# Two-layer hybrid decoder trunk: second-half operands of the way up made in chunks on VectorE, a third pair of weight columns begun early, and products added in PSUM

## The chip, the cores and the metric

The kernel runs on one core of a Trainium2 chip. The engines are TensorE (PE in the profile, with PEld for its weight loads), VectorE (DVE), ScalarE (ACT), GpSimd (POOL) and SyncE (SP), which issues nearly all transfers. The metric is the device time of one execution in microseconds (us), lower is better. Before the change it is 2558.94 us, the median of 3 runs from 2552.66 to 2560.61.

## What is computed

The reference is a decoder trunk of two layers over 1024 positions and 1024 features in float32. Each layer adds a mixer, then a SwiGLU feed-forward block, then a gated embedding. The change touches the feed-forward block alone, in both layers:

```python
def swiglu(h, w_gate, w_up, w_down):
    return (jax.nn.silu(h @ w_gate) * (h @ w_up)) @ w_down
...
h = h + swiglu(rmsnorm(h, g_ffn[layer]), w_gate[layer], w_up[layer], w_down[layer])
```

`w_gate` and `w_up` are 1024 x 2816, `w_down` is 2816 x 1024. The two products with `w_gate` and `w_up` are called the way up here, the one with `w_down` the way down.

## The kernel before

**Numbers.** Every float32 operand of a matmul is split in two parts that TensorE takes in a faster format: hi, a rounded copy made by ScalarE (line 146), and lo, the rest, a subtraction (line 147, on VectorE unless an engine is named). A product of two split operands is three matmuls (`mm3`, lines 205 to 207): hi by hi, hi by lo, lo by hi.

**The way up as a 2 x 2 block product with seven products in place of eight.** The positions form two halves of 512, the 1024 features two halves of 512, and the 2816 columns two halves of 1408, that is 11 columns `i` of 128 in each half. For one `i` and one of gate and up (a *column* below, `d` in the code) four output tiles of 128 x 512 are made, called 11, 12, 21 and 22, by the Winograd scheme: sums and differences of the four weight quarters (units 1 to 7 in `w_seven`) times sums and differences of the four operand quarters (`XC[1]` to `XC[7]`). One product is 4 feature tiles x 3 matmuls = 12 matmuls of 128 x 128 by 128 x 512, into one PSUM bank (`prod`, line 520). A layer has 22 columns (11 gate, 11 up) and 154 products. A gate column and its up column make a pair.

**Operands.** `XC[1]` and `XC[2]` depend only on the first half of the positions; they are ready before the way up begins. `XC[3]` to `XC[7]` also need the second half, whose norm factor `R[1]` is ready only some products into the way up: the two matmul groups `rs` and `Rb` of that norm run between the first products. `second_half` (line 470) then scales the eight second-half tiles (`normed`, line 437), makes the differences and splits 20 operands. Some of that is on VectorE (lines 483 and 485 and most lower halves), some on GpSimd (lines 488 and 495, four lower halves of `XC[4]` and two of `XC[3]`).

**Order.** Because of this wait, `ffn_up` (line 501) begins two pairs, four columns (called a0 to a3 here: gate and up of i = 0, gate and up of i = 1), with the two products that need only the first half: `p1` (its result is copied from PSUM by ScalarE, line 574) and `p2` (added to that copy by VectorE into output tile 11). `second_half` is written between them. Then each of the four gets its other weight units (`w_seven`) and its products 6, 3, 7, 5, 4 (`p6` and `rest`). From i = 2 on every column does 1, 6, 2, 3, 7, 5, 4 in one go. After every product an add on VectorE takes its bank: `u` lines 526 and 586, `sg` line 535 for gate, `act` line 540 for up. A gate tile then gets its SiLU on ScalarE (line 536), an up tile is multiplied with the gate tile on GpSimd (line 542), and `operands` stores the tiles and four differences of them (line 554, GpSimd, tiles `at`) to device memory for the way down.

**Weights.** `w_seven` loads four quarters of 256 KB, which wait for one of six buffers `raw`; GpSimd makes s1, s3, s2 and s4 (lines 184, 186, 188, 193); ScalarE and VectorE split seven units into eight pairs of buffers `whi` and `wlo`. A `raw` buffer is free again when its unit is split, a `whi` buffer when its product is done. For a0 to a3 `w_first` has made units 1 and 2 already.

**Buffers around it.** PSUM has six banks for products. Six temporaries `t` of 128 x 512 hold `p1`, `u`, `t2` and others. `slot` names fixed places; the gate tiles `sg` and the differences `at` share places 56 to 63, the up tiles stand in 64 to 68.

Instructions keep their order within an engine; which order that is, a planner fixes beforehand from the order of the program and its own estimate of durations, so a later instruction may be put ahead of one that it expects to be held up. At run time an engine waits at an instruction until what it needs is there.

Of the kernel before, what the change touches and what calls it, by code (L numbers as in the profile page):

```python
# [11 lines left out]
F32 = mybir.dt.float32  # L12
# [4 lines left out]
ALU = mybir.AluOpType  # L17
# [4 lines left out]
P = 128  # L22
# [24 lines left out]
class Build:  # L47
# [125 lines left out]
    def w_seven(self, w, c0, c1, name, u=None):  # L173
# [15 lines left out]
        u[6] = self.w_halves(s2, name)  # L189
        if not have:  # L190
            u[2] = self.w_halves(a12, name)
        s4 = a12
        tt(out=s4, in0=a12, in1=s2, op=ALU.subtract)
        u[3] = self.w_halves(s4, name)
        u[7] = self.w_halves(s3, name)
        u[5] = self.w_halves(s1, name)
        u[4] = self.w_halves(a22, name)
        return u

    def mm3(self, ps, a, b, first, last):

        mm = self.nc.tensor.matmul
        mm(ps, a[0], b[0], start=first, stop=False)  # L205
        mm(ps, a[0], b[1], start=False, stop=False)  # L206
        mm(ps, a[1], b[0], start=False, stop=last)  # L207

    def part_mm(self, ps, unit, op, first, last):
        n = len(unit)  # L210
        for k in range(n):
            self.mm3(ps, unit[k], op[k], first and k == 0, last and k == n - 1)
        self.tick()

    def ws_mm(self, ps, unit, kt, op, order=None):
# [125 lines left out]
def trunk(ctx, tc, x, p, positions, g_mix, g_ffn, g_ple, ev_w_in, ev_w_conv, ev_g_v, ev_w_s,  # L341
# [85 lines left out]
    def mixer_out(w, mix, res_d, h_d, gcol, order=None, begun={}, then=None):  # L427
# [40 lines left out]
        free = iter(list(range(32, 54)) + list(range(16, 32)) + [54, 55])  # L468

        def second_half():  # L470
            def made(key, x, eng):
                i = next(free)
                t = B.slots2(i, next(free), "xc")
                B.split(t[0], t[1], x, eng)
                XC[key].append(t)

            ks = range(4)
            t2s = []
# [12 lines left out]
            for k in ks:  # L491
                made(7, h[1][k], nc.vector)
            for k in ks:
                c = h[0][k + 4]
                nc.gpsimd.tensor_tensor(out=c, in0=c, in1=t2s[k], op=ALU.subtract)
                made(5, h[0][k], nc.vector)
            for k in ks:
                made(4, h[0][k + 4], nc.gpsimd)
        return XC, second_half

    def ffn_up(l, XC, second_half, act_d, behind):
# [2 lines left out]
        sg, act = {}, {}  # L504
        c2 = lambda i: slice(i * P, (i + 1) * P)

        def start(i, up, first=False):
            d = {"i": i, "up": up, "w": (w_gate, w_up)[up][l]}
            if first:
                d["u"] = B.w_first(d["w"], c2(i), "gu"[up])  # L510
            else:
                seven(d)
            return d
# [5 lines left out]
        def prod(d, k):  # L519
            ps = B.ps(f"p{k}")  # L520
            B.part_mm(ps, d["u"][k], XC[k], True, True)
            return ps

        def plus(a, b, name):
            t = B.tmp(name)
            nc.vector.tensor_tensor(out=t, in0=a, in1=b, op=ALU.add)
            return t

        def out(d, key, a, b):

            i, n = d["i"] + (half if key[0] == "2" else 0), int(key[1]) - 1
            j = int(key[0]) * 2 - 2 + n
            if not d["up"]:
                s = sg[i, n] = B.slot(56 + (d["i"] % 2) * 4 + j, F32, "sg")
                nc.vector.tensor_tensor(out=s, in0=a, in1=b, op=ALU.add)
                nc.scalar.activation(s, s, AF.Silu)
                return
            t = B.slot(68 if j == 0 and d["i"] % 2 else 64 + j, F32, "act")
            act[d["i"], key] = t
            nc.vector.tensor_tensor(out=t, in0=a, in1=b, op=ALU.add)  # L540
            last = d["i"] == half - 1
            (nc.vector if last else nc.gpsimd).tensor_tensor(  # L542
                out=t, in0=t, in1=sg[i, n], op=ALU.mult
            )
            operands(d["i"], key)

        def operands(i, key):


            keep = lambda k, t: nc.sync.dma_start(act_d[k][i], t)  # L550
            spare = lambda j: B.slot(56 + (i + 1) % 2 * 4 + j, F32, "at")

            def minus(t, a, b):
                nc.gpsimd.tensor_tensor(out=t, in0=a, in1=b, op=ALU.subtract)
                return t

            if key == "22":
                keep(2, act[i, "22"])
            elif key == "12":
                keep(1, act[i, "12"])  # L560
                act[i, "t1"] = minus(spare(1), act[i, "11"], act[i, "12"])
                keep(5, act[i, "t1"])
            elif key == "21":
                b = act[i, "21"]
                keep(3, b)
                t2 = minus(spare(2), b, act[i, "t1"])
                keep(6, t2)
                keep(7, minus(act[i, "11"], b, act[i, "11"]))
                keep(4, minus(spare(3), act[i, "22"], t2))

        def p1(d):
            a = prod(d, 1)
            d["p1"] = B.tmp("p1")
            nc.scalar.copy(d["p1"], a)  # L574
# [19 lines left out]
        ahead = []  # L594
        for i in range(2):
            ds = [start(i, up, True) for up in range(2)]
            for d in ds:
                p1(d)
            if i == 0:
                second_half()  # L600
            for d in ds:
                p2(d)
            ahead += ds
        for d in ahead:
            seven(d)
            p6(d)
            rest(d)
        for i in range(2, half):
            for up in range(2):
                d = start(i, up)  # L610
                p1(d)
                p6(d)
                p2(d)
                rest(d)

    half = NFF // 2
# [1290 lines left out]
```

## Time and profile before

| | |
|---|---|
| time, median of 3 runs | 2558.94 us (2552.66 to 2560.61) |
| the profiled execution's time | 2558.38 us |
| its span | 2556.7 us |
| way up of layer 0, first product to first matmul of the way down | 353.9 to 800.0 us |
| way up of layer 1 | 1738.2 to 2183.8 us |
| 256 KB loads of `w_gate` and of `w_up` | 96 each, median 3.1 and 2.9 us from issue to landing |

The page gives for each engine its busy time, share of the span and number of instructions. The waits of an engine are lines "who <- for whom: us in total, times, longest". A row of the timeline is start, duration, engine, line, operation, output and inputs, count, and in brackets the idle time before it with what ended it. A matmul's duration is longer than its distance to the next, since matmuls overlap. A row of the windows is a stretch, its length, and the busy time and count of PE, PEld, DVE, ACT and POOL, then the granted clock, the share of the DMA engines and GB/s.

### The profile page before, as it was taken

How to read it: one execution, taken by the hardware profiler on the slowest of the kernel's cores; microseconds unless marked ns; L12 is line 12 of the kernel's file. 1: busy time of each engine (PE TensorE's matmuls, PEld its weight loads, DVE VectorE, ACT ScalarE, POOL GpSimd, SP SyncE). 2: the span in 40 equal slices, each digit the busy share in tenths (PEclk: the TensorE clock that was granted, in tenths of full speed). 3: DMA queues.
4: the chain of work that ended last, by engine and by line, in shares of the span. 5: the costliest groups of instructions: out<-in, count | busy, mean ns of one | idle time of the engine just before them, and what ended most of it. 6: DMA issues, size and time to landing. Idle time of an engine off the chain costs nothing.

```text
span 2556.7 us, 34220 instructions
## 1 busy us (share of the span) xinstructions
PE 2451.1 (96%) x11510; PEld 2017.8 (79%) x11510; DVE 1565.3 (61%) x2935; ACT 977.5 (38%) x1869; POOL 1007.8 (39%) x918
## 2 busy tenths in 40 slices
PE   8999998999999988999999999997999999988999
PEld 6878876788888776788888788886888888876777
DVE  6863487555556667676775466468565455676732
ACT  5322342333224434444454455543233233444421
POOL 3451146565552554212221122126655554255300
PEclk9999999999999998999999999998999999998999
DMA  4221532333327657553455733162323324766731
GB/s 145 91 74 49 158 120 87 109 111 98 111 93 230 220 188 232 177 176 92 110 149 154 195 97 105 46 184 69 127 91 113 110 92 135 233 222 204 262 107 39
DMA packets 352736, 345.53 MB, mean 135 GB/s; under 512 B 23691, under 2 KB 245232, under 8 KB 352560
## 3 DMA queue, kind: packets, MB, share of 16 engines
q1 hardware_dynamic: 352064, 343.00, 43.2%
q8 instruction: 91, 1.49, 0.2%
q0 software_dynamic: 464, 0.33, 0.1%
q14 instruction: 85, 0.70, 0.1%
q10 hardware_dynamic: 32, 0.01, 0.0%
HBM read 251.51 MB, written 91.75 MB: 134 GB/s over the span
## 4 chain that ended last, share of the span: by engine, by line
PE 67%; DVE 7%; DMA 4%; issue 2%; POOL 2%; ACT 1%; SPq 0%; DVEq 0%; POOLq 0%; ACTq 0%
PE p L205 10%; PE p L206 10%; PE p L207 9%; PE pd L205 4%; PE pd L206 3%; PE pd L207 3%; DMA rd<-in_w_down 3%; PE O L1795 2%; PE ppg L207 2%; PE ppg L205 2%; PE ppg L206 2%; PE PT L1837 1%; PE po L205 1%; PE po L206 1%; PE po L207 1%
## 5 line engine op out<-in xcount | busy, mean ns | idle before, releaser
L205 PE MATMUL pd<-acth,hd 128*128 128x512 f32 x616 | 248.5, 403 | 41.2 <-DVE res L690 29.3
L147 DVE TENSOR_TENSOR lu<-ru,hu 128x512 fp32r<-128x512 f32 x138 | 128.2, 930 | 210.8 <-ACT hu L146 210.5
L206 PE MATMUL pd<-actl,hd 128*128 128x512 f32 x616 | 246.2, 400 | 0.0
L207 PE MATMUL pd<-acth,ld 128*128 128x512 f32 x616 | 245.2, 398 | 0.0
L205 PE MATMUL p<-xch,hg 128*128 128x512 f32 x440 | 177.3, 403 | 21.1 <-ACT p L574 15.1
L275 POOL TENSOR_TENSOR S<-S,sq 128x512 f32<-128x512 f32 x62 | 89.1, 1436 | 274.3 <-ACT sq L273 273.2
L146 ACT CAST hu<-ru 128x512 fp32r<-128x512 f32 x138 | 82.9, 619 | 274.7 <-POOL ru L188 173.2
L206 PE MATMUL p<-xcl,hg 128*128 128x512 f32 x440 | 175.7, 399 | 2.7 <-DVE xcl L147 2.7
L205 PEld LDWEIGHTS pd<-acth,hd 128*128 128x128 f32 x616 | 119.7, 194 | 71.4 <-DVE res L690 32.5
L207 PE MATMUL p<-xch,lg 128*128 128x512 f32 x440 | 174.8, 399 | 0.2 <-DVE lg L147 0.2
L207 PE MATMUL p<-xch,lu 128*128 128x512 f32 x440 | 172.9, 393 | 0.0
L205 PE MATMUL p<-xch,hu 128*128 128x512 f32 x440 | 172.9, 393 | 0.0
L206 PE MATMUL p<-xcl,hu 128*128 128x512 f32 x440 | 172.6, 392 | 0.0
L147 DVE TENSOR_TENSOR ld<-rd,hd 128x512 fp32r<-128x512 f32 x110 | 99.5, 905 | 82.1 <-ACT hd L146 81.7
L147 DVE TENSOR_TENSOR actl<-ra,acth 128x512 fp32r<-128x512 f32 x154 | 142.3, 928 | 11.9 <-ACT acth L146 11.7
L147 DVE TENSOR_TENSOR lg<-rg,hg 128x512 fp32r<-128x512 f32 x132 | 110.8, 840 | 61.9 <-ACT hg L146 61.5
L146 ACT CAST hg<-rg 128x512 fp32r<-128x512 f32 x132 | 80.8, 619 | 177.1 <-POOL rg L188 56.6
L207 PEld LDWEIGHTS pd<-acth,ld 128*128 128x128 f32 x616 | 119.6, 194 | 25.8
L206 PEld LDWEIGHTS pd<-actl,hd 128*128 128x128 f32 x616 | 119.9, 195 | 24.6
L542 POOL TENSOR_TENSOR act<-act,sg 128x512 f32<-128x512 f32 x80 | 118.9, 1498 | 18.3 <-DVE act L540 9.7
L146 ACT CAST hd<-rd 128x512 fp32r<-128x512 f32 x110 | 68.4, 622 | 149.5 <-POOL rd L651 51.1
L205 PEld LDWEIGHTS p<-xch,hg 128*128 128x128 f32 x440 | 84.7, 193 | 42.3 <-ACT p L574 16.0
(552 smaller groups left out, 6787.6 us busy)
## 6 DMA issues: line engine op xcount, KB each, us to landing
rd<-in_w_down SPq DMA_DIRECT2D x198, 256.0 KB, 3.4
ra<-act SPq DMA_DIRECT2D x154, 256.0 KB, 3.1
rg<-in_w_gate SPq DMA_DIRECT2D x96, 256.0 KB, 3.1
ru<-in_w_up SPq DMA_DIRECT2D x96, 256.0 KB, 2.9
act<-act SPq DMA_DIRECT2D x88, 256.0 KB, 2.0
act<-at SPq DMA_DIRECT2D x66, 256.0 KB, 2.1
rpg<-in_w_ple_gate SPq DMA_DIRECT2D x48, 256.0 KB, 3.0
rwo<-in_ev_w_out SPq DMA_DIRECT2D x32, 256.0 KB, 2.8
```

The lines of the kernel that those rows point to most:

```text
L146: self.nc.scalar.copy(hi, src)
L147: (eng or self.nc.vector).tensor_tensor(out=lo, in0=src, in1=hi.bitcast(F32), op=ALU.subtract)
L205: mm(ps, a[0], b[0], start=first, stop=False)
L206: mm(ps, a[0], b[1], start=False, stop=False)
L207: mm(ps, a[1], b[0], start=False, stop=last)
L275: eng.tensor_tensor(out=st[n], in0=st[n], in1=sq, op=ALU.add)
L542: (nc.vector if last else nc.gpsimd).tensor_tensor(out=t, in0=t, in1=sg[i, n], op=ALU.mult)
L1795: nc.tensor.matmul(O[h][:, b * DV : (b + 1) * DV], t[:, j * P : (j + 1) * P], V[h // 2][:, kb, (h % 2) * DV : (h % 2 + 1) * DV], start=kb ...
L1837: nc.tensor.transpose(pt[:, j * P : (j + 1) * P], e[:, j * P : (j + 1) * P], ident)
```

## The change

It has these parts:

- `second_half` becomes a generator of nine chunks. All its subtractions and splits use VectorE (and ScalarE for the hi parts); none uses GpSimd. Chunks 1 to 4 make `XC[6]`, two more `XC[7]`, one each `XC[5]`, `XC[4]`, `XC[3]`. The caller runs a chunk after nearly every first product.
- A third pair (i = 2, `third`) is begun early as well. Order of the first products: p1 of a0 to a3, p2 of a0 to a3, then p1, p1, p2, p2 of the third pair. Its p1 copies and its tile 11 are kept in `raw` buffers and stored to device memory (`early`), and loaded again when the pair is finished, after a3.
- p2 is accumulated onto p1's PSUM bank, after ScalarE has copied p1 out of it; tile 11 is read straight from that bank (`out11`). Product 4 is accumulated onto product 7's bank and product 3 onto product 5's, each after VectorE has read that bank. Two adds per column go.
- Products come in the order 6, 7, 5, 4, 3; `w_seven` makes unit 3 last; the four differences in `operands` are all made after tile 12, now the last one.

```diff
@@ second_half
+            minus = lambda o, a, b: nc.vector.tensor_tensor(out=o, in0=a, in1=b, op=ALU.subtract)
             for k in ks:
                 normed(1, k)
                 normed(1, k + 4)
-                a, b, d = h[0][k], h[1][k], h[1][k + 4]
-                nc.vector.tensor_tensor(out=a, in0=b, in1=a, op=ALU.subtract)
+                a, b, c, d = h[0][k], h[1][k], h[0][k + 4], h[1][k + 4]
+                minus(a, b, a)
                 t2 = B.tmp("t2")
-                nc.vector.tensor_tensor(out=t2, in0=d, in1=a, op=ALU.subtract)
-                t2s.append(t2)
-                made(6, t2, nc.vector)
-                nc.gpsimd.tensor_tensor(out=b, in0=d, in1=b, op=ALU.subtract)
+                minus(t2, d, a)
+                made(6, t2)
+                minus(c, c, t2)
+                yield
             for k in ks:
-                made(3, h[1][k + 4], (nc.vector, nc.gpsimd)[k % 2])
-            for k in ks:
-                made(7, h[1][k], nc.vector)
-            for k in ks:
-                c = h[0][k + 4]
-                nc.gpsimd.tensor_tensor(out=c, in0=c, in1=t2s[k], op=ALU.subtract)
-                made(5, h[0][k], nc.vector)
-            for k in ks:
-                made(4, h[0][k + 4], nc.gpsimd)
+                minus(h[1][k], h[1][k + 4], h[1][k])
+                made(7, h[1][k])
+                if k % 2:
+                    yield
+            for key, x in ((5, h[0][0:4]), (4, h[0][4:8]), (3, h[1][4:8])):
+                for t in x:
+                    made(key, t)
+                yield
...
@@ ffn_up
+        def out11(d, t):
+            if not d["up"]:
+                nc.scalar.activation(t, d["X"], AF.Silu)
+                sg[d["i"], "11"] = t
+            else:
+                nc.vector.tensor_tensor(out=t, in0=d["X"], in1=sg[d["i"], "11"], op=ALU.mult)
+                act[d["i"], "11"] = t
...
+        def p1(d, t):
+            d["X"], d["p1"] = prod(d, 1), t
+            nc.scalar.copy(t, d["X"])
         def p2(d):
-            out(d, "11", prod(d, 2), d["p1"])
+            prod(d, 2, d["X"])
         def p6(d):
-            d["u2"] = plus(prod(d, 6), d["p1"], "u2")
+            u2 = d["p1"]
+            nc.vector.tensor_tensor(out=u2, in0=prod(d, 6), in1=u2, op=ALU.add)
         def rest(d):
-            u2 = d["u2"]
-            u4 = plus(prod(d, 3), u2, "u4")
-            p7 = prod(d, 7)
-            nc.vector.tensor_tensor(out=u2, in0=p7, in1=u2, op=ALU.add)
+            u2 = d["p1"]
+            pa = prod(d, 7)
+            u3 = B.tmp("u3")
+            nc.vector.tensor_tensor(out=u3, in0=pa, in1=u2, op=ALU.add)
             if d["up"] and d["i"] == half - 1:
                 behind()
-            p5 = prod(d, 5)
-            out(d, "22", p5, u2)
-            out(d, "12", p5, u4)
-            out(d, "21", prod(d, 4), u2)
+            pb = prod(d, 5)
+            out(d, "22", pb, u3)
+            prod(d, 4, pa)
+            out(d, "21", pa, u2)
+            prod(d, 3, pb)
+            out(d, "12", pb, u2)
...
+        for d in ahead:
+            first(d)
+        for j, d in enumerate(ahead):
+            p1(d, B.tmp("p1"))
+            if j:
+                next(more)
+        for j, d in enumerate(ahead):
+            p2(d)
+            if j < 2:
+                first(third[j])
+            next(more)
+        seven(ahead[0])
+        for d, t in zip(third, early):
+            p1(d, raw("p1"))
+            nc.sync.dma_start(t, d["p1"])
+            next(more, None)
+        for d in third:
+            p2(d)
+            next(more, None)
+            out11(d, raw("o11"))
+        nc.sync.dma_start(early[2], act[2, "11"])
+        for _ in more:
+            pass
+        for d in ahead:
+            out11(d, spot(d, "11"))
+        for j, d in enumerate(ahead):
+            if j:
+                seven(d)
+            p6(d)
+            rest(d)
+        for d, t in zip(third, early):
+            seven(d)
+            d["p1"] = load(t, "p1")
+            p6(d)
+            if d["up"]:
+                t = act[2, "11"] = spot(d, "11")
+                nc.sync.dma_start(t, early[2])
+            rest(d)
+        for i in range(3, half):
             for up in range(2):
                 d = start(i, up)
-                p1(d)
+                seven(d)
+                p1(d, B.tmp("p1"))
                 p6(d)
                 p2(d)
+                out11(d, spot(d, "11"))
                 rest(d)
```

`first(d)` is `w_first` of the column, `seven(d)` is `w_seven`, `spot` names the slot of an output tile. In `prod(d, k, ps)` a given bank is accumulated onto.

More of the change, by code (lines that the diff above doesn't have):

```diff
@@ L505, in ffn_up, with start, first @@
         c2 = lambda i: slice(i * P, (i + 1) * P)
[L507 to L513, printed above, removed]
+        def start(i, up):
+            return {"i": i, "up": up, "w": (w_gate, w_up)[up][l]}
+        def first(d):
+            d["u"] = B.w_first(d["w"], c2(d["i"]), "gu"[d["up"]])
         def seven(d):
@@ L604, in ffn_up @@
-        for d in ahead:
-            seven(d)
+            pb = prod(d, 5)
[4 more added lines that the diff above has]
+            out(d, "12", pb, u2)
+        more = second_half()
+        ahead = [start(i, up) for i in range(2) for up in range(2)]
+        third = [start(2, up) for up in range(2)]
+        raw = lambda name: B.wp.tile([P, HT], F32, tag="raw", name=B.name(name), bufs=RAW)
+        early = [dp.tile([P, HT], F32, name=B.name("early")) for _ in range(3)]
```

85 lines of the change are left out of this document (34 added, 51 removed).

## The prediction

> **What bounds the kernel now.** I read the page first, then TensorE's waits, then the timeline of the way up.
>
> ```profile
> PE 2451.1 (96%) x11510; PEld 2017.8 (79%) x11510; DVE 1565.3 (61%) x2935; ACT 977.5 (38%) x1869; POOL 1007.8 (39%) x918
> ```
>
> TensorE is the bound. Nothing in the change removes a matmul, so the most it can win is TensorE's idle and slow time inside the two ways up (one per layer). TensorE's waits name it:
>
> ```profile
> PE p L205 <- ACT p L574: 15.1, 2, 7.6
> ...
> PE p L205 <- DVE sg L535: 6.0, 2, 3.0
> ...
> PE p L206 <- DVE xcl L147: 2.7, 2, 1.7
> ...
> PE p L205 <- DVE u L526: 0.9, 1, 0.9
> ```
>
> All but the last come twice, once per layer. The timeline gives their places (start, duration, then in brackets the idle time before it and who ended it):
>
> ```profile
> 353.88 0.39 PE L205 MATMUL p<-xbh,hg 128*128 128x512 f32 x1
> ...
> 357.61 1.02 PE L282 MATMUL rs<-ones_f,S 128*128 128x1 f32 x8 [0.85 <-DVE S L275]
> ...
> 365.39 0.39 PE L205 MATMUL p<-xbh,hu 128*128 128x512 f32 x1
> ...
> 378.76 0.39 PE L207 MATMUL p<-xbh,lu 128*128 128x512 f32 x1
> 386.72 0.80 PE L205 MATMUL p<-xch,hg 128*128 128x512 f32 x1 [7.57 <-ACT p L574]
> 387.31 0.63 PE L206 MATMUL p<-xcl,hg 128*128 128x512 f32 x1
> 387.74 0.63 PE L207 MATMUL p<-xch,lg 128*128 128x512 f32 x1
> ...
> 409.40 0.39 PE L205 MATMUL p<-xch,hu 128*128 128x512 f32 x1
> ...
> 1738.21 0.39 PE L205 MATMUL p<-xbh,hg 128*128 128x512 f32 x1
> ...
> 1794.44 0.39 PE L205 MATMUL p<-xch,hu 128*128 128x512 f32 x1
> ```
>
> The stage of layer 0 begins at 353.88, that of layer 1 at 1738.21. The fourth product starts at 365.39; product 8 starts its last matmul at 378.76, 59 matmuls on: 13.37 / 59 = 0.2266 us each, 2.72 us per product of 12. At 409.40 (and 1794.44) the second weight column, a1, starts product 6. By then 13 products are done: two first products of each of four columns, and five more of a0.
>
> Their price undisturbed: 13 x 2.72 = 35.4, plus what the norm of the second half inserts. That is 365.39 - 353.88 = 11.51 for three products (8.16): 3.35. Together 38.7. Measured are 55.5 in layer 0 and 56.2 in layer 1, so **16.8 and 17.5 us are lost** in idle time and slow matmuls (0.63 for 0.39). That is the prey.
>
> Why it idles: each column of a pair holds PSUM banks, six in all, and the fourth copy of product 1 (L574) and the adds L535/L540 come late.
>
> ```profile
> 384.52 1.66 ACT L146 CAST xch<-h 128x512 fp32r<-128x512 f32 x3 [1.17 <-POOL h L495]
> 386.09 0.57 ACT L574 COPY p<-p 128x512 f32<-128x512 f32 x1
> ...
> 364.59:398.20 33.61, 22.11 (x89) 17.16 (x87) 33.61 (x31) 15.61 (x26) 23.71 (x14) 0.90 0.03 9
> ...
> 364.59 1.41 DVE L437 SCALAR_TENSOR_TENSOR h<-h,vec,R 128x512 f32<-128x512 f32 x2 [0.66 <-ACT R L317]
> ...
> 390.61 1.75 DVE L147 TENSOR_TENSOR xcl<-t,xch 128x512 fp32r<-128x512 f32 x1
> 392.28 5.99 DVE L147 TENSOR_TENSOR xcl<-h,xch 128x512 fp32r<-128x512 f32 x8
> 398.20 0.68 DVE L535 TENSOR_TENSOR sg<-p,p 128x512 f32<-128x512 f32 x1
> ...
> 393.75 1.56 POOL L147 TENSOR_TENSOR xcl<-h,xch 128x512 fp32r<-128x512 f32 x1 [1.94 <-ACT xch L146]
> ```
>
> The copy stands behind casts that wait for POOL. In the windows row (PE, PEld, DVE, ACT, POOL: busy and count) VectorE is full for 33.61 us with 31 operations, 1.08 each, while POOL runs 14. Beside a POOL operation one takes 1.75; in the run of eight, with POOL's single L147 beside one of them, it is (5.99 - 1.7) / 7 = 0.61. So second-half operands cost VectorE about 0.6 alone and 1.7 beside POOL.
>
> **The change part by part.**
>
> *Operands on VectorE alone.* 44 operations (30 of the 31, whose last is already an add, and POOL's 14): 8 norms at 0.66 and 36 at 0.60 are 26.9 us with POOL quiet, against 33.6 now. The operands of product 6 are the first four chunks, 4 x (2 x 0.66 + 4 x 0.60) = 14.9 us.
>
> *Third pair begun early.* Four more products, 10.9 us, stand ahead of product 6 of a0. R comes about when it does now: 364.6. TensorE reaches product 6 at 353.9 + 3.35 + 12 x 2.72 = 389.9; its operands are there at 364.6 + 14.9 + 2.4 (four lower halves of the third pair's first weights) = 381.9. Product 7's follow at 386.7. The rest of the queue is 12 halves for products 5, 4, 3 (7.2) and five of a0's weights (3.0): 396.9, wanted at 389.9 + 4 x 2.72 = 400.8. So it fits by 4 us while POOL is quiet. POOL is not: `w_seven` of a0 and of a1 gives it eight subtractions here, each costing VectorE up to 1.75 - 0.61 = 1.1: 0 to 8.8.
>
> The Trainium skill, "SBUF — State Buffer", section "Who interferes with whom", says that a VectorE instruction with two SBUF inputs and a GpSimd one that reads SBUF block each other for the whole instruction; it would make this up to 8 x 1.29 = 10.3, and the rows show 1.1 a pair, a little less.
>
> *The supply of a1's weights.* In the trace they follow directly on a0's lower halves:
>
> ```profile
> 400.59 0.86 DVE L147 TENSOR_TENSOR lg<-rg,hg 128x512 fp32r<-128x512 f32 x1
> ...
> 406.35 1.29 POOL L188 TENSOR_TENSOR ru<-su,ru 128x512 f32<-128x512 f32 x1
> ```
>
> a0's halves (from 400.59) free the raw buffers, a1 is loaded, POOL ends its s2 at 407.64, TensorE starts at 409.40. After the change 17 products are done by then, undisturbed at 389.9 + 13.6 = 403.5, and a0's halves come before the operands of 4 and 3, near 391 to 399. So a1's product 6 lies between 403.5 and 409.4: a new wait of 0 to 5.9 per layer. I take 3.0, the middle.
>
> *A smaller gain.* S L275 takes long because POOL works on a0's weights:
>
> ```profile
> 355.69 1.77 DVE L275 TENSOR_TENSOR S<-S,sq 128x512 f32<-128x512 f32 x1
> ...
> 355.30 1.61 POOL L188 TENSOR_TENSOR rg<-sg,rg 128x512 f32<-128x512 f32 x1
> ```
>
> Now the third pair's first loads take those buffers, POOL comes later, and the 0.85 of idle time (357.61) should go: 0 to 0.85 per layer, taken whole.
>
> *Products added in PSUM.* p2 is added onto p1's bank, p4 onto p7's, p3 onto p5's. Two VectorE adds per column go; on VectorE, idle in the steady part, they are worth nothing. But TensorE gets three new waits per column: p2 for the copy of p1, p4 for the add that reads p7, p3 for the add that reads p5, each with one product of 2.7 us between. In the trace these readers are often later:
>
> ```profile
> 496.09 0.39 PE L207 MATMUL p<-xch,lg 128*128 128x512 f32 x1
> ...
> 506.36 0.69 DVE L147 TENSOR_TENSOR lu<-ru,hu 128x512 fp32r<-128x512 f32 x1 [10.82 <-ACT hu L146]
> 506.97 0.68 DVE L526 TENSOR_TENSOR u<-p,p 128x512 f32<-128x512 f32 x1
> ...
> 512.63 0.39 PE L207 MATMUL p<-xbh,lu 128*128 128x512 f32 x1
> ...
> 519.76 0.58 ACT L574 COPY p<-p 128x512 f32<-128x512 f32 x1
> ...
> 650.70 0.39 PE L207 MATMUL p<-xch,lg 128*128 128x512 f32 x1
> ...
> 656.52 0.68 DVE L526 TENSOR_TENSOR u<-p,p 128x512 f32<-128x512 f32 x1
> ...
> 667.24 0.39 PE L207 MATMUL p<-xbh,lu 128*128 128x512 f32 x1
> ...
> 669.37 0.58 ACT L574 COPY p<-p 128x512 f32<-128x512 f32 x1
> ```
>
> Product 6 of a gate column ends at 496.5, its add starts at 506.97, 10.5 late, behind a lower half of the next column that waits for POOL. Later in the stage it is 656.52 - 651.1 = 5.4. The copy of an up column's p1 is 519.76 - 513.0 = 6.8 late, later 669.37 - 667.6 = 1.7. Today six banks absorb this. Behind a waiting p2 or p4 stands all the rest of TensorE's queue, in order, and with it the next column's casts that wait for weight buffers. With the change p4's wait allows the first add some 6.2 us (three products less about two operations), the copy 2.2 (2.7 less its 0.58). So the steady part passes, by 0.8 and 0.5 us; the early columns, at 10.5 and 6.8, would stall by 4.3 and 4.6. A stall moves TensorE back and lets the others catch up, so it is paid about once, not per column. Between 0 and, with the slots of `at` (whose stores VectorE waits for, 4.6 at the longest) repeating it for a2 and the third gate column, 4.3 + 4.6 + 4.6 = 13.5 per layer. I take 4.5, nearer to one of them.
>
> ```profile
> DVE sg L535 <- DMA act<-at: 9.2, 2, 4.6
> ```
>
> *Moved with it.* SP issues ten more transfers per layer (four loads of weights, three stores, three loads back). The stores of `early` stand on SP ahead of a1's loads and wait for the copy and for out11; those loads wait for a0's buffers at that point anyway, so nothing, or, if out11 is late, part of the 5.9 above. u3 of `w_seven` goes last as p3 does; nothing. At the end of the stage `behind` gets three products of cover for two; nothing.
>
> **Sum.** Removed: 16.8 + 17.5, the 0.9 of u L526, 2 x 0.85 = 36.9. Added: 2 x (3.0 + 4.5) = 15. The profiled execution takes 2558.4 (span 2556.7); the median of the runs, 2558.9, is the same within their spread. 2558.4 - 36.9 + 15 = **2536.5**.
>
> A clock term could add to this. The trace shows it behind a short wait:
>
> ```profile
> 1783.28 0.80 PE L205 MATMUL p<-xch,hg 128*128 128x512 f32 x1 [3.00 <-DVE sg L535]
> ...
> 1788.59 0.63 PE L207 MATMUL p<-xch,lg 128*128 128x512 f32 x1
> ```
>
> After 3.00 us of idle the matmuls run at 0.63 for over 5 us, 0.2 us lost on each of some 13: 2.6. By the Trainium skill, "TensorE: Matmul & The Clock Gate", Part 1, the clock halves only after an idle window of about 3.4 us, so waits of the size I add would cost nothing beyond themselves. The trace disagrees; by the row a wait of 3 in each layer could cost 2 x 2.6 = 5.2 more. I leave it to the range.
>
> **The rivals.**
>
> *Only the four products are won.* The supply of a1 does not move: its product 6 starts at 409.4 as now, with 17 products done for 13. Then each layer wins 4 x 2.72 = 10.9 less the 4.5: 2 x 6.4 = 13, so 2545; with 8 of later stalls, 2553. For it: POOL's s2 is 1.8 us ahead of TensorE now. Against: a0's halves are queued earlier.
>
> *VectorE is not alone.* POOL's eight subtractions spread over the stretch, and 44 operations at 1.08 take 47.5: 364.6 + 47.5 + 5.4 of weights = 417.5, wanted at 400.8. The wait is 16.7 per layer for the 3.0: 2536.5 + 27 = 2564. Against: eight POOL operations, not fourteen plus weights; the bound of 8.8 exceeds the 4 us of slack by 4.9.
>
> *Slower: the readers of PSUM.* If p2 or p4 waits in every pair from the fourth on, eight pairs in two layers, it decides from (21.9 + 9) / 16 = 1.9 us a pair, beyond margins of only 0.5 and 0.8. At 3.0 a pair it is 48 in place of the 9 taken: 2575. For it: the two late rows above, and the long wait of lu for hu, 10.82. Against: when the stall comes, POOL and ACT catch up, and a steady pair leaves VectorE half idle: 19.84 of 38.65 us, TensorE full.
>
> ```profile
> 609.80:648.45 38.65, 38.65 (x170) 31.54 (x169) 19.84 (x28) 11.76 (x21) 22.11 (x17) 1.00 0.32 103
> ```
>
> **How the numbers follow.** Forecast, 2519 to 2546: 0.57. Four products only, 2546 to 2556: 0.18. VectorE not alone, 2556 to 2566: 0.07. Slower by readers, above 2566: 0.18. About 0.3% (7.7 us) is what a measurement here can tell from no change: below 2551 is faster, above 2566.6 slower. Of the second case two thirds are faster: 0.57 + 0.13 = 0.70; slower 0.18; same 0.12. The range goes from 2519 (36.9 without any new wait gives 2521.5) up to 2562, leaving out the slower case and little else.
>
> **What would show it.** Right: product 6 of a0 near 390 with no wait for ACT p, second-half operands at 0.6 on VectorE, POOL without L147 and L488/L495 there, a1's product 6 between 403 and 409. Wrong: TensorE waits `p <- ACT p` (copy of p1) or `p <- DVE` of the adds, in many small pieces after 480; then the steady pair is longer than 38.65. A longer stretch of weights on POOL between 380 and 400 would show the third case.

## Result and profile after

The change makes the kernel **slower**, by 1.1%: 2589.95 us, the median of 4 runs (2585.33 to 2594.59), against 2559.78 for the kernel before (4 runs). The ratio is 1.0112 with a 95% interval of [1.0075, 1.0149]. Forecast were 2536.5 us and a range that ended at 2562.

The page of the changed kernel, busy time, share of the span and instructions of each engine:

```profile
PE 2464.4 (95%) x11510; PEld 2025.4 (78%) x11510; DVE 1522.1 (59%) x2895; ACT 983.3 (38%) x1869; POOL 946.0 (37%) x870
```

VectorE and GpSimd have less to do than before (DVE 1522.1 for 1565.3, POOL 946.0 for 1007.8), as the change says, and the span is still 29.9 us longer (2586.6 for 2556.7). TensorE's instructions are the same 11510. So the time went into TensorE's waits and slow matmuls. The windows cut each way up at the matmul with which a1's product 6 begins (busy PE, PEld, DVE, ACT, POOL, then granted clock, DMA share, GB/s). Before, layer 0, in 13 products and the other 141:

```profile
353.88:409.40 55.52, 41.88 (x167) 31.96 (x166) 50.43 (x61) 21.88 (x37) 38.17 (x24) 0.91 0.10 29
409.40:800.00 390.60, 389.68 (x1693) 317.51 (x1692) 213.09 (x305) 123.65 (x215) 216.74 (x158) 1.00 0.37 116
```

After, in 17 products and the other 137, and one steady pair:

```profile
355.31:413.93 58.62, 51.51 (x215) 41.48 (x214) 43.87 (x80) 26.92 (x47) 15.63 (x9) 0.91 0.20 59
413.93:815.73 401.80, 384.57 (x1646) 310.02 (x1645) 201.44 (x267) 121.75 (x205) 210.71 (x150) 0.99 0.36 114
660.55:700.66 40.11, 38.93 (x169) 31.46 (x168) 19.42 (x25) 11.96 (x20) 21.07 (x16) 1.00 0.31 99
```

The way up of layer 0 takes 58.62 + 401.80 = 460.4 us for 446.1, that of layer 1 460.4 for 445.6: 14.3 + 14.8 = 29.1 of the profiled execution's 30.2 (2588.56 for 2558.38). Two things are in it.

**The front won, less than forecast.** 17 products in 58.6 are, less four undisturbed ones (10.9), 13 in 47.7; before they took 55.5. That is a gain of 7.8.

**The rest lost three times that.** Before, 141 products took 390.60, 2.77 each, with TensorE busy for 389.68 of it. 137 of them would be 379.5. They took 401.80: 22.3 lost in layer 0. In layer 1 it is 401.9 against 389.4 / 141 x 137 = 378.4: 23.5. TensorE's waits say where:

```profile
PE p L205 <- ACT p L579: 32.3, 18, 6.7
...
PE p L205 <- DVE sg L532: 9.9, 4, 4.5
PE p L205 <- DVE u L592: 5.7, 2, 2.9
```

L579 is ScalarE's copy of product 1, and 18 waits for it are nine in each layer: one of 6.7, and eight short ones, one for each pair of the steady part. The timeline (start, duration, in brackets the idle time and what ended it) shows one of each kind:

```profile
384.55 0.39 PE L207 MATMUL p<-xbh,lu 128*128 128x512 f32 x1
391.64 0.79 PE L205 MATMUL p<-xbh,hg 128*128 128x512 f32 x1 [6.71 <-ACT p L579]
392.23 0.63 PE L206 MATMUL p<-xbl,hg 128*128 128x512 f32 x1
...
425.35 0.76 PE L205 MATMUL p<-xch,hu 128*128 128x512 f32 x1 [2.85 <-DVE u L592]
...
448.10 0.47 PE L205 MATMUL p<-xch,hg 128*128 128x512 f32 x1 [4.42 <-DVE sg L532]
...
657.76 0.39 PE L207 MATMUL p<-xbh,lg 128*128 128x512 f32 x1
...
660.55 0.40 PE L207 MATMUL p<-xch,lg 128*128 128x512 f32 x1
662.13 0.50 PE L205 MATMUL p<-xbh,hg 128*128 128x512 f32 x1 [1.18 <-ACT p L579]
```

In the front, the third pair's first p2 waits 6.71 (391.64). Product 4 of a1 waits 2.85 for the add that reads its bank (425.35), product 3 of a2 4.42 (448.10). Then every gate column's p2 waits: product 1 ends with the matmul of 657.76, product 6 with that of 660.55, p2 starts at 662.13. The longer waits are followed by slow matmuls, 0.63 for 0.39, seven each after the last two, which costs some 0.2 each. Together: 2.85 + 4.42 + 8 x 1.46 (40.11 - 38.65, the pair after and before) + 14 x 0.2 = 21.8 of the 22.3.

Why is the copy late? ScalarE's and GpSimd's timeline at that p2, after:

```profile
660.97 0.62 ACT L146 CAST hu<-ru 128x512 fp32r<-128x512 f32 x1 [5.11 <-PE p L207]
661.50 0.58 ACT L579 COPY p<-p 128x512 f32<-128x512 f32 x1
...
655.32 3.00 POOL L539 TENSOR_TENSOR act<-act,sg 128x512 f32<-128x512 f32 x2
658.39 1.29 POOL L560 TENSOR_TENSOR at<-act,act 128x512 f32<-128x512 f32 x1
659.65 1.29 POOL L188 TENSOR_TENSOR ru<-su,ru 128x512 f32<-128x512 f32 x1
```

and at the same place before:

```profile
647.91 0.39 PE L207 MATMUL p<-xbh,lg 128*128 128x512 f32 x1
...
648.34 0.59 ACT L574 COPY p<-p 128x512 f32<-128x512 f32 x1 [2.32 <-PE p L207]
...
653.93 1.29 POOL L188 TENSOR_TENSOR ru<-su,ru 128x512 f32<-128x512 f32 x1
655.26 1.14 ACT L146 CAST hu<-ru 128x512 fp32r<-128x512 f32 x2 [6.33 <-POOL ru L188]
```

Before, the copy came as soon as product 1 had ended, and the cast of the next up column's unit 6, which waits for GpSimd's L188, stood behind it. After, the two have changed places on ScalarE: the cast stands first, and the copy waits with it, until 3.35 us past the end of product 1 (658.15). GpSimd does L188 behind multiplications of the column that has just ended (L539) and the first difference (L560). It is no later with L188 than it was: before, L188 ended 6.9 after product 1 (655.22 for 648.30), now 2.8. What is new is that the copy stands behind it; which part of the change made the planner order it so was not tried. The cast's row names TensorE, since product 6 ended at the same time as L188 (660.94); in e3 below the same cast follows L188 while product 6 is still running.

### The profile page after: what moved, and what is told of

It reads as the page before. It is cut to its first block, busy times and chain, and to the rows that moved or that the text cites. A ratio compares the mean times of both kernels' runs of the same rounds, so it can differ in the third digit from the quotient of the medians.

```text
span 2586.6 us, 34050 instructions
## 1 busy us (share of the span) xinstructions
PE 2464.4 (95%) x11510; PEld 2025.4 (78%) x11510; DVE 1522.1 (59%) x2895; ACT 983.3 (38%) x1869; POOL 946.0 (37%) x870
## 4 chain that ended last, share of the span: by engine, by line
PE 72%; DVE 10%; DMA 6%; issue 5%; POOL 4%; ACT 2%; SPq 0%; POOLq 0%; DVEq 0%; ACTq 0%
PE p L205 9%; PE p L206 9%; PE p L207 9%; DMA rd<-in_w_down 3%; PE pd L205 3%; PE pd L206 3%; PE pd L207 3%; PE O L1835 2%; PE ppg L205 2%; PE ppg L206 2%; PE ppg L207 2%; PE po L205 2%; PE po L206 2%; PE po L207 2%; PE PT L1877 1%
## 5 line engine op out<-in xcount | busy, mean ns | idle before, releaser
L147 DVE TENSOR_TENSOR lu<-ru,hu 128x512 fp32r<-128x512 f32 x138 | 150.0, 1090 | 108.5 <-ACT hu L146 108.5
L147 DVE TENSOR_TENSOR actl<-ra,acth 128x512 fp32r<-128x512 f32 x154 | 137.7, 898 | 13.8 <-ACT acth L146 13.6
L147 DVE TENSOR_TENSOR ld<-rd,hd 128x512 fp32r<-128x512 f32 x110 | 95.5, 868 | 83.3 <-ACT hd L146 83.1
L539 POOL TENSOR_TENSOR act<-act,sg 128x512 f32<-128x512 f32 x60 | 94.1, 1580 | 105.6 <-DVE act L532 105.6
L147 DVE TENSOR_TENSOR lg<-rg,hg 128x512 fp32r<-128x512 f32 x132 | 99.6, 759 | 47.7 <-ACT hg L146 47.7
L146 ACT CAST acth<-ra 128x512 fp32r<-128x512 f32 x154 | 94.4, 617 | 33.6 <-DMA ra<-act 23.4
```

The costliest lines, as they stand in the source:

```text
L146: self.nc.scalar.copy(hi, src)
L147: (eng or self.nc.vector).tensor_tensor(out=lo, in0=src, in1=hi.bitcast(F32), op=ALU.subtract)
L539: (nc.vector if last else nc.gpsimd).tensor_tensor(out=t, in0=t, in1=sg[d["i"], key], op=ALU.mult)
```

## Experiments

All times of the way up below are of the profiled executions, layer 0 / layer 1. Ratios are to the kernel before, measured on the same chip (medians 2558.06 to 2559.78).

| kernel | median, us | ratio [95%] | way up, us |
|---|---|---|---|
| before | 2559.78 | | 446.1 / 445.6 |
| the change | 2589.95 | 1.0112 [1.0075, 1.0149] | 460.4 / 460.4 |
| e1, p2 in its own bank | 2566.14 | 1.0024 [1.0001, 1.0046] | 450.2 / 449.6 |
| e2, p2 one product later | 2567.26 | 1.0033 [1.0017, 1.005] | 449.3 / 448.8 |
| e3, products 4 and 3 in own banks | 2555.44 | 1.0001 [0.998, 1.0021] | 443.2 / 443.9 |
| e4, e1 and e3 | 2551.65 | 0.9966 [0.9951, 0.998] | 441.0 / 443.1 |
| f1, e4 without the third pair | 2531.26 | 0.9895 [0.9863, 0.9928] | 435.2 / 435.3 |
| f2, e4, a0's units made later | 2547.20 | 0.9955 [0.9936, 0.9974] | 438.3 / 438.8 |
| f3, e4, a0's subtractions on VectorE | 2543.74 | 0.994 [0.9917, 0.9963] | 435.5 / 435.8 |
| f4, before with VectorE alone | 2551.73 | 0.997 [0.994, 0.9999] | 439.8 / 439.1 |
| g1, f1 and f3's edit | 2533.37 | 0.9897 [0.9883, 0.991] | 435.1 / 435.1 |
| g2, e4 with both edits of f2 and f3 | 2548.02 | 0.9959 [0.9946, 0.9973] | 436.9 / 437.2 |
| g3, the change without the third pair | 2585.11, one run | | 460.9 / 459.4 |
| g4, f1 with the second half in one piece | 2534.78 | 0.991 [0.9896, 0.9923] | 435.8 / 436.2 |

### The adding in PSUM: e1 to e4

e1 gives p2 a bank of its own again, from i = 3 on, and adds on VectorE.

```diff
-        def p6(d):
-            u2 = d["p1"]
-            nc.vector.tensor_tensor(out=u2, in0=prod(d, 6), in1=u2, op=ALU.add)
+        def p6(d, own=False):
+            u2 = B.tmp("u2") if own else d["p1"]
+            nc.vector.tensor_tensor(out=u2, in0=prod(d, 6), in1=d["p1"], op=ALU.add)
+            d["u2"] = u2
+
+        def p2_own(d, t):
+            nc.vector.tensor_tensor(out=t, in0=prod(d, 2), in1=d["p1"], op=ALU.add)
...
-                p6(d)
-                p2(d)
-                out11(d, spot(d, "11"))
+                p6(d, True)
+                p2_own(d, spot(d, "11"))
```

> From column pair i = 3 on, product 2 goes to a PSUM bank of its own and VectorE adds the copy of product 1, as before the change; all else as in the changed kernel. Theory (the copy of a gate column's product 1 stands on ScalarE behind the next up column's cast, which waits for GpSimd's s2; TensorE waits for the copy at product 2): the 1.35 us gap in front of each gate column's product 2 goes in 8 pairs, a steady pair falls from 40.1 us to 38.7, each way up from 460.4 to about 449, the kernel to about 2566. Rival (the next wait, product 4 for the add that reads product 7's bank, takes its place): the pair stays near 40, the time near 2588.

e2 keeps p2 on the bank of p1 but puts it after product 7 (order 1, 6, 7, 2, 5, 4, 3 from i = 3 on), with unit 7 split ahead of unit 2. It tells the wait for the copy from the adding as such.

```diff
                 p6(d)
-                p2(d)
-                out11(d, spot(d, "11"))
-                rest(d)
+                rest(d, lambda d: (p2(d), out11(d, spot(d, "11"))))
```

> As the changed kernel, but from pair i = 3 on the order of products is 1, 6, 7, 2, 5, 4, 3 in place of 1, 6, 2, 7, 5, 4, 3, so that two products and not one stand between product 1 and the accumulation onto its bank. Theory: the copy comes 3.9 us after product 1's end and now has 5.5, so the gap goes: pair 38.7, way up about 449, kernel about 2566, as with the bank of its own. Rival (any accumulation onto a bank that was just read costs TensorE, wherever it stands): the gap moves with product 2 and the pair stays at 40.1.

Both take the eight short waits away, and the steady pair is 38.65 again in both. What is left of the waits for L579 is the front's, one per layer. In e1:

```profile
PE p L205 <- ACT p L579: 13.4, 2, 6.7
```

In e2 the copy is as late as in the changed kernel, behind the same cast, and nothing waits for it:

```profile
654.53 0.62 ACT L146 CAST hu<-ru 128x512 fp32r<-128x512 f32 x1 [5.11 <-POOL ru L188]
655.06 0.58 ACT L579 COPY p<-p 128x512 f32<-128x512 f32 x1
```

So adding p2 onto the bank costs nothing by itself. What costs is that p2 follows with only one product between while the copy stands behind a cast: 10 to 12 us per layer.

e3 gives products 4 and 3 banks of their own.

```diff
-            prod(d, 4, pa)
-            out(d, "21", pa, u2)
-            prod(d, 3, pb)
+            out(d, "21", prod(d, 4), u3)
+            nc.vector.tensor_tensor(out=u2, in0=prod(d, 3), in1=u2, op=ALU.add)
             out(d, "12", pb, u2)
```

In the kernel, the last line takes product 5's bank as before.

> As the changed kernel, but products 4 and 3 go to banks of their own in every column, with the VectorE adds of before. Theory: the waits of a1's product 4 (2.85 us) and of a2's product 3 (4.42 us) and the slow matmuls behind them go, about 10 us of each layer; the 1.35 us gaps in front of product 2 stay: way up about 450, kernel about 2569. Rival (these waits stand for late weights, and TensorE waits for the next column's weights as long as it did for the banks): the two waits reappear in front of a2's product 6 and later, way up near 460.

e4 has the edits of e1 and e3.

> Both of these: product 2 in a bank of its own from i = 3 on, products 4 and 3 in banks of their own everywhere. What is left of the change is the third pair begun early, VectorE alone for the second half, and product 2 added in PSUM for the three first pairs. Theory: both savings add, way up 438 to 440, against 446 before, and the kernel near 2546, faster than before by 0.5%. Rival (the front itself is what costs): not below 446, kernel at 2559 or above.

e3 took away the waits of a1 (2.85) and a2 (4.42), as expected; a shorter one of 2.08, for a bank that a late add (L532) frees, came at a3's product 4. But the short waits of the steady part went too, all but the first of each layer (1.91 and 0.77), and that was not expected: 443.2 where 450 was. Its timeline shows why. In its order L188 stands ahead of the last multiplication and of L560:

```profile
643.32 1.29 POOL L539 TENSOR_TENSOR act<-act,sg 128x512 f32<-128x512 f32 x1
645.30 1.30 POOL L188 TENSOR_TENSOR ru<-su,ru 128x512 f32<-128x512 f32 x1 [0.69 <-DVE lu L147]
646.56 1.30 POOL L539 TENSOR_TENSOR act<-act,sg 128x512 f32<-128x512 f32 x1
...
646.63 0.62 ACT L146 CAST hu<-ru 128x512 fp32r<-128x512 f32 x1 [2.77 <-POOL ru L188]
647.16 0.58 ACT L579 COPY p<-p 128x512 f32<-128x512 f32 x1
```

The copy is now 1.02 us late, product 6 takes 2.7, and p2 finds its bank free. The cast starts 0.03 after L188 ends, 2.3 before product 6 does. That confirms the chain (multiplications, L188, cast, copy, p2) from its other end: it was broken at GpSimd, by an order that the edit did not aim at. e4 adds little to e3, as this chain was gone already: 441.0 and 443.1, where 438 to 440 was expected.

### The front: f1 to f3, g1 to g3

f1 is e4 without the third pair: `third` is empty, nothing is kept in `early`, and the steady loop begins at i = 2.

```diff
-        third = [start(2, up) for up in range(2)]
+        third = []
...
-            if j < 2:
-                first(third[j])
...
-        nc.sync.dma_start(early[2], act[2, "11"])
...
-        for i in range(3, half):
+        for i in range(2, half):
```

> As e4_all_own, but without the third pair: two pairs are begun early, as before the change. Theory (the third pair's four products fill 10.9 us in which TensorE would wait, less the 6.7 us that it then waits for the copy of the third pair's first product): the way up grows from 441 to 443 (e4) to about 446, the kernel from 2552 to about 2559. Rival (the third pair brings nothing, since its own copy wait eats it): way up stays at 441 to 443.

f2 is e4 with `seven(ahead[0])` behind the third pair's product 1, so that a0's casts do not stand ahead of its copies.

```diff
-        seven(ahead[0])
         for d, t in zip(third, early):
             p1(d, raw("p1"))
             nc.sync.dma_start(t, d["p1"])
             next(more, None)
+        seven(ahead[0])
```

> As e4_all_own, but the weights of a0 (w_seven) are written behind the third pair's products 1, so that ScalarE gets the copies of these products ahead of a0's casts, which wait for GpSimd. Theory: the 6.7 us wait and the slow matmuls behind it go, a1's product 6 starts 52 to 54 us into the stage and not 58.6, the way up is about 436, the kernel about 2541. Rival (a0's weights come later and TensorE waits for them as long): product 6 of a1 at 58 or later, way up 441 or more.

f3 is e4 with the four subtractions of a0's `w_seven` on VectorE in place of GpSimd.

```diff
-        seven(ahead[0])
+        seven(ahead[0], nc.vector)
```

> As e4_all_own, but the four subtractions of a0's weights are on VectorE and not on GpSimd. Theory (GpSimd's first of them took 5.2 us because VectorE held it off; ScalarE's casts and behind them the copy wait for this): the wait of 6.7 us for the copy falls to about 3, a1's product 6 starts near 55, way up about 438. Rival (the copy is late for the number of casts ahead of it): wait and way up as in e4, 441 to 443.

They aim at the wait of 6.71. In the changed kernel the third pair's first copy stands on ScalarE behind casts of a0's units, and these wait for GpSimd (its and ScalarE's timeline):

```profile
378.91 5.23 POOL L184 TENSOR_TENSOR sg<-rg,rg 128x512 f32<-128x512 f32 x1 [15.16 <-ACT xch L146]
384.21 1.27 POOL L186 TENSOR_TENSOR rg<-rg,rg 128x512 f32<-128x512 f32 x1
385.56 1.26 POOL L188 TENSOR_TENSOR rg<-sg,rg 128x512 f32<-128x512 f32 x1
...
386.86 1.14 ACT L146 CAST hg<-rg 128x512 fp32r<-128x512 f32 x2 [6.83 <-POOL rg L188]
...
391.02 0.57 ACT L579 COPY p<-p 128x512 f32<-128x512 f32 x1
```

A subtraction that takes 1.27 elsewhere took 5.23. f3 halves the wait, and the way up falls to 435.5 and 435.8:

```profile
387.66 0.50 PE L205 MATMUL p<-xbh,hg 128*128 128x512 f32 x1 [3.54 <-ACT p L579]
```

What is left of the wait is another queue: the copy now stands behind casts of second-half operands and a SiLU with a table load of 1.28.

f2 lets the third pair through, but the same units are then late for a0's product 6. The front takes 59.1, not the 52 to 54 expected:

```profile
396.11 0.80 PE L205 MATMUL p<-xch,hg 128*128 128x512 f32 x1 [7.34 <-ACT hg L146]
```

f1 was expected to lose by having four products less in the front; it is the **best of all** in time, with g1 and g4 close to it. Its windows, 13 products and the other 141:

```profile
354.30:398.46 44.16, 39.37 (x168) 29.82 (x166) 38.92 (x71) 21.64 (x37) 15.56 (x8) 1.00 0.12 36
398.46:789.50 391.04, 390.20 (x1693) 317.49 (x1694) 227.00 (x314) 128.17 (x216) 215.38 (x151) 1.00 0.36 115
```

and of TensorE's waits in that way up the longest and the one of a1's product 6:

```profile
PE p L205 <- DVE act L550: 1.1, 1, 1.1
...
PE p L205 <- ACT hu L146: 0.9, 1, 0.9
```

The clock is 1.00 in both windows and no matmul runs at 0.63. Against e4 (58.6 for 17, or 47.7 for 13; then 382.3 for 137) the front gains 3.5 and the rest, at 382.3 + 10.9 = 393.2 for 141, 2.2: the third pair begun early, with its weights as in e4, costs some 6 us in layer 0, 8 in layer 1.

g1 puts a0's subtractions on VectorE in f1 too, g2 puts f2's and f3's edits together in e4, and g3 is the changed kernel with the third pair taken out as in f1.

> f1_no_third (no third pair, no adding in PSUM but for product 2 of the two first pairs), with the four subtractions of a0's weights on VectorE as in f3. Theory (what holds the first products back is GpSimd's late s2, held off by VectorE): 13 products are done at 42 us and not 44.2, way up about 433, kernel about 2527. Rival (without the third pair GpSimd makes these weights in good time, and four more operations lengthen VectorE's queue): 44 to 46 us, way up 435 to 437.

> With the third pair: e4_all_own with both f2 (a0's weights written behind the third pair's products 1) and f3 (their subtractions on VectorE). Theory A (the third pair pays once neither the copy nor the weights are late): 17 products are done at 52 us or earlier, way up at most 433, under f1's 435.2. Theory B (the third pair does not pay, since without it the 13 products are already within 6 us of undisturbed): 17 products at 55 us or later, way up 435 or more.

> The changed kernel with all products added in PSUM as it has them, but without the third pair. Theory (the adding in PSUM costs by itself some 22 us of each way up, behind the front): 13 products at about 44 us as in f1, and the rest about 410, way up 452 to 457. Rival (it only costs because the third pair makes the supply of weights late): way up 437 to 442.

g1 gains nothing over f1 (435.1): without the third pair TensorE's waits are the same in both, none over 1.1. g2 still waits 6.6 in the front, now for a0's casts, and stays at 436.9. So f3 is the third pair at its best, and its way up is 0.4 and 0.7 longer than that of g1, which has the same edit without the pair: in none of the four forms tried does the third pair shorten the way up. In time f2, f3 and g2 are 0.5 to 0.6% above f1, but in f3 the way up does not show it. Its profiled execution is 6.9 us longer than f1's (2537.02 for 2530.14), and 4.6 of this stand between the two ways up, a stretch that no edit touches and that varies from 934.6 to 946.3 us among the profiled executions.

g3 was to tell whether the adding in PSUM costs by itself or only beside the third pair. It costs by itself: the way up takes 460.9, with the short waits back in the steady part and this in the front:

```profile
399.45 0.80 PE L205 MATMUL p<-xch,hu 128*128 128x512 f32 x1 [7.89 <-ACT hu L146]
```

Here the first nine matmuls of a1's product 6 stand ahead of a0's last two products in TensorE's order and wait for a1's weights, so 13 products take 52.0; in f1, with banks of their own, a0's go first and 13 take 44.2. The theory's 452 to 457 was missed by that wait; its other 141 products, in 408.8, are the 410 that it expected.

### VectorE alone and the chunks: f4 and g4

f4 is the kernel before with the four GpSimd uses in `second_half` turned to VectorE, nothing else.

```diff
-                made(3, h[1][k + 4], (nc.vector, nc.gpsimd)[k % 2])
+                made(3, h[1][k + 4], nc.vector)
...
-                made(4, h[0][k + 4], nc.gpsimd)
+                made(4, h[0][k + 4], nc.vector)
```

> The kernel before with one part of the change alone: second_half's differences and splits all on VectorE, none on GpSimd. Theory (an operation costs VectorE 0.6 us with GpSimd quiet and 1.7 beside it): VectorE's stretch falls from 33.6 to about 27 us for 44 operations in place of 30, TensorE's waits in front of a1's product 6 from 16.8 to about 10, way up about 440, the kernel near 2547. Rival (14 more operations in VectorE's queue cost as much as the quiet brings): way up 446 or longer.

g4 is f1 with all nine chunks run after the second product 1.

```diff
-            if j:
-                next(more)
+            if j == 1:
+                for _ in more:
+                    pass
```

> f1_no_third, but the second half's operands are written in one piece behind the second product, as before the change, and not in chunks. Theory (the planner orders by readiness, so the place in the program does little; what f1 gains over f4, the kernel before with VectorE alone, is the bank saved in each of the first four columns): 13 products at 44 to 45 us, way up 435 to 436. Rival (the chunks are what sets f1 apart from f4): 48 to 49 us, way up about 439.

f4 wins 6.3 and 6.5 us per layer, as expected: 13 products in 49.1 and 48.0. Its time came to 2551.73, where 2547 was expected. Its window over the stretch in which VectorE was full before:

```profile
366.00:399.00 33.00, 25.93 (x102) 20.79 (x101) 32.94 (x52) 17.36 (x29) 3.61 (x3) 0.84 0.06 17
```

52 operations on VectorE in 32.94 us, 0.63 each, where the kernel before had 31 in 33.61. g4 is as fast as f1 (the way up is 0.6 and 0.9 longer, the intervals overlap), so the chunks add nothing that these runs can tell in time. What takes f4's 439.8 to f1's 435.2 lies between: p2 added in PSUM for the first four columns, and the new order of products, weight units and differences. These were not tried apart.

## Why the prediction was wrong

**What was right.** The prey: f1 does 13 products in 44.2 where the prediction had 55.5 for the kernel before and 38.7 undisturbed, and loses nothing in the rest. VectorE alone: operations at 0.6, and product 6's operands in time. The last lower half of its four chunks, by the forecast 17.3 us after the norm begins (364.6 to 381.9), was done at 381.18, 16.2 after it (364.95), and no matmul waited for it:

```profile
364.95 1.42 DVE L437 SCALAR_TENSOR_TENSOR h<-h,vec,R 128x512 f32<-128x512 f32 x2 [0.66 <-ACT R L317]
...
380.50 0.68 DVE L147 TENSOR_TENSOR xcl<-t,xch 128x512 fp32r<-128x512 f32 x1
```

The smaller gain came as well: TensorE's `rs` has no idle time before it.

```profile
358.04 0.95 PE L282 MATMUL rs<-ones_f,S 128*128 128x1 f32 x8
```

And the early columns stalled: 2.85 at product 4, where 4.3 was priced. The 4.42 has the size of the 4.6 priced for a copy, but by luck: it is product 3's wait for an add. Together they make 7.3, where the sum took 4.5 for one of them.

**The step that failed: "So the steady part passes, by 0.8 and 0.5 us".** The lateness of the readers was taken from rows of the kernel before, where the copy of a gate column's product 1 came at once, and only the up column's was looked at. But the change gives the planner another program, and in the order that it wrote for it the gate's copy stands behind a cast that waits for GpSimd: 3.35 late against an allowance of 2.2. "A stall moves TensorE back and lets the others catch up, so it is paid about once" failed with it. The same chain is rebuilt in every pair, tied to the last products of the column before, so it is paid eight times per layer at 1.46. The term of 4.5 per layer was in truth 22.3 and 23.5, 36.8 too little in two layers. e1 and e2 show this cause from the side of TensorE, e3 from that of GpSimd.

**The term that was mis-sized: 3.0 for "the supply of a1's weights".** The forecast had 17 products done at 49.6 into the stage, with 3.0 added and 0.85 taken off 51.8. Measured are 58.6 and 58.4. a1's weights were in time; what came instead is the 6.71 for the third pair's copy and the slow matmuls after it. About half of that wait stems from a GpSimd operation that VectorE held up: with the operation gone from GpSimd, in f3, it is 3.54. The prediction charged the meeting of the two engines to VectorE (0 to 8.8, covered by 4 us of slack) and not to GpSimd, whose product ScalarE's whole queue waited for. The miss, 58.6 and 58.4 for 51.8, is 6.7 per layer, 13.4 in all. The two misses make 50 of the 52 us between forecast and profiled execution (2588.56 - 2536.5).

**The rivals.** "Slower: the readers of PSUM" is what happened, with p2's wait in every pair from the fourth on. Its price was 1.46 a pair, below the 1.9 at which it alone would decide. The kernel is slower because the single waits of a1 and a2 and that of the front stand beside it. "VectorE is not alone" was refuted by the DVE row above. "Only the four products are won" did not come either: a1's product 6 started 58.6 into the stage, and the 10.9 were lost before it.

**What the third pair was worth.** The prediction's 10.9 per layer for four more products was taken from a loss that the other part had already removed. With VectorE alone and the new order, only 44.2 - 38.7 = 5.5 us of idle time were left to fill (f1), and the four products cost 5.8 and 7.8 more than they filled (e4 against f1), at best 0.4 and 0.7 (f3 against g1). Which of their copies, loads and casts costs how much, the runs don't tell.

## What to carry to other kernels

When a result is added onto a PSUM bank that another engine must read first, ask what stands ahead of that reader on its engine in the *new* order; a lateness that was read from the old trace holds only for the old order. Leave two products between the read and the next write (e2), or spend a bank and an add on an idle engine (e1). When two parts of a change fill the same idle time, price the second one on what the first leaves, and run each alone: here the change without its third pair, and with nothing added in PSUM but product 2 of the first four columns, won 1.0%, and the whole lost 1.1%.

## What the runs showed of the hardware

**Who is held up varies.** Before, VectorE and GpSimd side by side slowed VectorE: 1.75 for a lower half. In the changed kernel VectorE kept its pace and GpSimd stood still:

```profile
378.69 0.68 DVE L477 TENSOR_TENSOR t<-h,h 128x512 f32<-128x512 f32 x1
379.30 0.68 DVE L147 TENSOR_TENSOR lu<-ru,hu 128x512 fp32r<-128x512 f32 x1
...
381.10 1.89 DVE L477 TENSOR_TENSOR h<-h,h 128x512 f32<-128x512 f32 x3
389.06 1.90 DVE L147 TENSOR_TENSOR xcl<-h,xch 128x512 fp32r<-128x512 f32 x3 [6.08 <-ACT xch L146]
```

VectorE went on at one operation per 0.60 us until 382.99, and L184, begun at 378.91, ended at 384.14, 1.15 after that. In g3 one such operation took 6.41, and the wait of 7.89 came behind it; in f1 one took 6.42, with no harm, as nothing on TensorE waited for it long. In both it ended 1.1 after the last of a run of lower halves (L147), while VectorE was at an operation that reads one of its two inputs from PSUM (L550). The Trainium skill, "SBUF — State Buffer", section "Who interferes with whom", says that a VectorE instruction with two SBUF inputs and a GpSimd one that reads SBUF exclude each other and that the order of issue decides who is blocked. The trace agrees that one of them stands still, and adds that GpSimd can lose the place to some seven VectorE instructions in a row: it got on only when VectorE paused or read from PSUM.

**The clock changes on a grid of 3.41 us, and the length of a wait alone does not decide.** In the way up of layer 0, waits of 2.03 (e4), 2.85, 4.42 and 6.71 us were followed by matmuls at 0.63, but so was one of 1.00 in g4, with 0.92 and 0.72 just before it. Waits of 1.18, of 1.87 (f3) and even of 3.12 (e2) were not. In every trace the granted clock changes only at multiples of 3.41 us from an earlier change. The windows cut at this grid tell the cases apart. In e4 the whole wait of 2.03 lies in one stretch (busy PE 1.38 of 3.41), and the next is granted half the clock:

```profile
448.55:451.96 3.41, 1.38 (x6) 0.83 (x6) 2.19 (x3) 2.00 (x4) 1.80 (x2) 1.00 0.10 37
451.96:455.37 3.41, 3.41 (x9) 2.66 (x9) 2.79 (x6) 2.05 (x5) 0.00 (x0) 0.50 0.65 173
```

In e2 the wait of 3.12 falls on two stretches, which leave TensorE idle for 1.7 and 1.4, and the clock stays:

```profile
419.98:423.39 3.41, 1.70 (x8) 1.04 (x6) 1.15 (x2) 1.80 (x4) 2.77 (x3) 1.00 0.00 0
423.39:426.80 3.41, 2.00 (x9) 1.68 (x10) 3.41 (x7) 0.90 (x2) 0.00 (x0) 1.00 0.54 156
426.80:430.21 3.41, 3.41 (x17) 2.81 (x16) 0.26 (x1) 0.00 (x0) 2.56 (x3) 1.00 0.53 152
```

So it goes in all stretches at full clock in the ways up of the 14 traces: after up to 1.94 us of idle time in a stretch the next one kept the clock, after 1.98 and more it got half, with one exception (1.76, in g4). The Trainium skill, "TensorE: Matmul & The Clock Gate", Part 1, names an idle window of about 3.4 us; the grid agrees, but some 2 us of idle time inside one such window were enough here.
